# Sums of weight blocks in DRAM, requested at other places of a two-layer trunk kernel

## The chip, the cores and the metric

The kernel runs on one core of a Trainium2 chip. The metric is device time in microseconds of one execution. Three runs of the kernel before took 1001.95, 1002.94 and 1003.8 us (median 1002.94). A further execution was profiled: it took 1001.16 us, of which the trace covers a span of 999.4 us.

## The reference

Two layers, each a feed-forward block (FFN), a mixer and a second FFN, on 256 tokens of width 1024, all in float32:

```
def hybrid_layer(x, ...):
    x = x + 0.5 * swiglu(rms_norm(x, ffn1_norm), ffn1_w_gate_up, ffn1_w_down)
    z = rms_norm(x, mix_norm) @ w_in              # u, q, k, v, gates
    y_pool = multiscale_pool(u, pool_w, pool_scale)
    y_attn = moba_attention(rope(rms_norm(q)), rope(rms_norm(k)), v)
    gates = sigmoid(gl + b_gate)
    x = x + (gates[0] * (y_pool @ w_branch_pool) + gates[1] * (y_attn @ w_branch_attn)) @ w_out
    x = x + 0.5 * swiglu(rms_norm(x, ffn2_norm), ffn2_w_gate_up, ffn2_w_down)
    return x
```

An FFN's gate and up matrix is 1024 x 5632, its down matrix 2816 x 1024.

## The kernel before

**Weights.** They lie in DRAM as units of 1 MB, each used once. `fetch` (L134) loads the next unit of a fixed plan into one of four `raw` buffers with a DMA from SP's queue (L143, or L193 in `sum_form`). ScalarE (ACT) then rounds it to `hi` (L209, L198), and VectorE (DVE) makes the rest `lo` (L210, L199), in two halves each, since TensorE (PE) multiplies float32 as split float32r parts. There are three sets of hi and lo buffers. A load is thus issued when an earlier unit is split, and a split when PE has done with a still earlier one: PE, ACT, DVE and SP's queue form a ring some seven units deep.

**Stages.** In order of time, by the profile: FFN 1 of layer 0 (base 0, "the first stage") with 22 up units to about 129 us and 11 down units to 184; the mixer of layer 0 (`mix`: q, k and v units, the pooling input u in `project_u`, eight gate units, four branch units, four output units) to about 336; FFN 2 of layer 0 (base FU) to 509; FFN 1 of layer 1 (base LU) to 678; the mixer of layer 1 to 830; FFN 2 of layer 1 (base LU + FU) to the end.

**Seven products for eight.** The three FFNs after the first compute some of their up units by a scheme with seven products in place of eight, on groups A, B and C of units (`FEED`; FU and LU + FU have A and C in the order TWO, LU has A, B and C in the order THREE). Its forms "7", "6", "5" and "4" are sums of quarters of weight units. The names 1, 2 and 3 are plain quarters. PE's products with forms write tiles `b`; ordinary units write `ps`.

**The sums.** Each of the four forms of a group is made in DRAM by two DMAs from GpSimd's queue (POOL, L183), "steps" below: a copy of 1 MB into a DRAM tile `f` (from the weights `w`, or from another form: `f<-f`), then a second DMA that adds 1 MB onto it (`accum_op`). Form 6 starts from 7, and 4 from 6, so some steps wait until earlier ones have landed. Seven groups make 56 steps, of which 14 are `f<-f`. `far_sums` puts them into the list `steps_left`, the first eight steps of a group being interleaved with the last three (`rest`) of the group before, across the borders of the stages too. `go_on` (L175) takes the next step and issues it; it makes the DMA wait for the last entry of `marks`, the DVE instruction that ended the unit of work just before. So where `go_on` is called sets when a step may start, and POOL, which issues in order, may be held further by the landing of an earlier step. When the list is empty, `go_on` does nothing.

**Places before.** Seven calls among the up units of the first stage (after units 8, 10, ..., 20), five among the down units (`far_at`: units 1, 3, 5, 7, 9), and in the mixer one after q, two after the rotary steps of q and k, eleven at the gates (two after gates 0, 1 and 2, one after each other), two at branch units and four at output units: 20 in a mixer, 32 before FFN 2 of layer 0. That FFN has 4 + 5, the next 2 + 5, and the last 8 fall into the mixer of layer 1.

**Pooling on POOL.** `pool_sums` runs on POOL between the steps (L857 to L862); its result is first read by DVE in `pool_diff` (L868) after gate 3.

Of the kernel before, what the change touches and what calls it, by code (L numbers as in the profile page):

```python
# [44 lines left out]
FU = NF + NF // 2 + 24  # L45
LU = FU + NF + NF // 2
# [14 lines left out]
def groups_of(base):  # L61
    return "AC" if FEED[base] is TWO else "ABC"
# [12 lines left out]
C_G1, C_GM, C_G2, C_BG, C_PS, NG = 0, 8, 16, 24, 40, 44  # L75
# [3 lines left out]
def trunk_kernel(ctx: ExitStack, tc: tile.TileContext, x_in, w_in, pw_in, qkn_in, rope_in, mask_in, band_in, out):  # L79
    nc = tc.nc  # L80
# [31 lines left out]
    def banks(pool, name):  # L112

        return pool.tile([P, 2, 2, S], F32, name=name, tag="mm" if pool is pmm else "at2")
# [13 lines left out]
    def unit():  # L128

        if not ahead:  # L130
            fetch()
        return ahead.pop(0)
# [17 lines left out]
    far, steps_left = {}, []  # L150

    def quadrant(base, g, q):

        n, kh = base + GROUPS[g] + (0 if q[1] == "1" else 2), int(q[0]) - 1
        return w_in[n:n + 2, :, kh * HALF:(kh + 1) * HALF].rearrange("u p c -> p u c")

    def two_rows(z):
        return z.rearrange("p (i c) -> p i c", i=2)

    def far_sums():  # L160

        rest = []
        for base in STAGES:
            for g in groups_of(base):
                one, two = ({z[0]: (base, g, z[0], z[i], kw) for z in SUMS}
                            for i, kw in ((1, {}), (2, {"accum_op": OP.add})))
                for z in one["7"], one["5"], two["7"]:
                    steps_left.append(z)
                    steps_left.extend(rest[:1])
                    rest = rest[1:]  # L170
                steps_left.extend((two["5"], one["6"]))
                rest = [two["6"], one["4"], two["4"]]
        steps_left.extend(rest)

    def go_on():  # L175

        if not steps_left:
            return
        base, g, f, src, kw = steps_left.pop(0)
        if not kw:  # L180
            far[f, g, base] = far_pool.tile([P, 2 * HALF], F32, name="f" + f, tag=f"{base}{g}{f}")
        src = two_rows(far[src, g, base]) if len(src) == 1 else quadrant(base, g, src)
        z = nc.gpsimd.dma_start(two_rows(far[f, g, base]), src, **kw)  # L183
        tc.add_manual_dep(z.ins, marks[-1].ins.name, mybir.DependencyInfo(
            mybir.DependencyClass.Sync, mybir.DependencyReason.DATA), reason="behind")
# [60 lines left out]
    def pair(w, t, other=None, at=0):  # L246

        ps = banks(pmm, "ps")
        columns(w, ps, range(at))
        if other:  # L250
            other()
        columns(w, ps, range(at, NK))
        drain(t, ps)
# [8 lines left out]
    def behind(z, other):  # L262

        tc.add_manual_dep(z.ins, other.ins.name, mybir.DependencyInfo(
            mybir.DependencyClass.NoSync, mybir.DependencyReason.DATA), reason="behind")
# [22 lines left out]
    x = gx[:, L * NG:L * NG + NK * S].rearrange("p (k s) -> p k s", s=S)  # L288
# [18 lines left out]
    for t in range(PAD - 1):  # L307
        g = min(g for g, w in enumerate(WINDOWS) if t < w - 1)
# [7 lines left out]
    def split_x(f, l, col):  # L316

        g = gain[:, l, col + f:col + f + 1]
        act(hx[:, f, 0, :], x[:, f, :], AF.Copy, scale=g)
        stt(hx[:, f, 1, :], x[:, f, :], g, hx[:, f, 0, :].bitcast(F32), op0=OP.mult, op1=OP.subtract)  # L320

    def square_x(f):

        if f == 0:
            act(acc, x[:, f, :], AF.Square)
        else:
            sq = small.tile([P, S], F32, name="sq", tag="sq", bufs=2)
            act(sq, x[:, f, :], AF.Square)
            tt(acc, acc, sq, op=OP.add)

    def prep(f, l, col):
        split_x(f, l, col)
        square_x(f)
# [83 lines left out]
    def bc2(a):  # L417
        return a.unsqueeze(1).to_broadcast([P, 2, a.shape[-1]])

    def ffn(after, n0=0, end=False, col=None, base=0, far_at=(), steps_at=()):  # L420
# [19 lines left out]
        def wide(n):  # L440
            m = n // 2
            if m not in abs_:
                k = len(abs_)
                if n0 and 3 <= k < 7:
                    if not more:
                        z = acts.tile([P, NK * GW + 4 * SHIFT], F32, name="ab", tag="gates")
                        more.extend(z[:, i * 4 * S:(i + 1) * 4 * S].rearrange("p (b a s) -> p b a s", b=2, s=S) for i in range(4))
                    abs_[m] = more.pop(0)
                else:
                    abs_[m] = wide_tile(k if k < 3 or not n0 else k - 4)  # L450
            return abs_[m][:, n % 2]
# [25 lines left out]
        if n0:  # L477
# [6 lines left out]
            for i in range(n0 + 1, NF + 1):  # L484
                if i < NF:
                    pair(unit(), wide(i))
                    fetch()
                    if i >= 8 and i % 2 == 0:
                        go_on()
                if i == NF or i % 3 != 1:  # L490
                    for n in range(done, NF if i == NF else min(done + 2, i - 1), 2):
                        scaled = post(n)
                        done = n + 2
                        if i == n0 + 1:
                            behind(scaled, drained[-1])
# [206 lines left out]
    def normed(pt, rt, name):  # L702
        z = acts.tile([P, 2, GW], F32, name=name, **({"tag": "v"} if name == "v" else {"tag": "tok", "bufs": 2}))
        for t in range(2):
            act(z[:, t, :], pt[:, t], AF.Copy, scale=rt[:, t:t + 1])
        return z
# [87 lines left out]
    def mix(l, after):  # L794
# [5 lines left out]
        pt = tokens()  # L800
        r = spread(*z)
        k = normed(pt, rt, "k")
        spare = acts.tile([P, 8 * GW], F32, name="spare", tag="ga")
        yk, pk = ([z[:, i] for i in range(4)] for z in (
            acts.tile([P, 4, 2, S], F32R, name=n, tag=t) for n, t in (("yk", "gc"), ("pk", "gd"))))
# [23 lines left out]
        def project_u():  # L829
            us = [unit() for _ in range(2)]  # L830
            for g in range(0, NW, 2):
                ps = banks(pmm, "ps")
                for k in range(NK):
                    for j in range(2):
                        chain(ps[:, j], *us[k // 4], k % 4 * 4 + g + j, hk[k], k == 0, k == NK - 1)
                z = uT[:, g:g + 2, PAD:]
                drain(z, ps)
                tt(z, z, bc2(r), op=OP.mult)

        pool = [gates[6 + g // 2][:, g % 2, :] for g in range(NW)]  # L840
        W = PAD + S
# [57 lines left out]
        rest = slice(3 * P, 4 * P)  # L899
# [45 lines left out]
        for h in range(NH):  # L945
            gate(h, *((lambda: score_two(h // 2), NK // 2) if h % 4 == 0 else ()))
            if h == 4:
                for p, y in enumerate(ys):
                    heads_end(p, y)
                known = soften_two()  # L950
            elif h < 2:
                soften(h)
            elif h % 4 == 2:
                turn_two(h // 4 * 2, (0, 1) if h > 4 else ())
            elif h == 3:
                pool_diff()
            open_gate(h)
            for _ in range(2 if h < 3 else 1):
                go_on()

        def branch(f, j, k0=0, k1=4):
# [40 lines left out]
        for f in range(4, NK):  # L1002
            if f % 2 == 0:
                ws.append(unit())
                go_on()
            for j in range(2):
                branch(f, j)
            if f == 5:
                fetch()
            mixed(f)  # L1010
        ws, sums = [], []

        def project(f, k0=0, k1=NK):
            if f % 2 == k0 == 0:
                ws.append(unit())
                go_on()
            if k0 == 0:
                sums.append(quarter("ps"))
            ps = sums[f][:, 0]
            chain3(ps, *ws[f // 2], f % 2 * 8 + k0, mk[k0:k1], k0 == 0, k1 == NK)  # L1020
            if k1 == NK:
                marks.append(tt(x[:, f, :], ps, x[:, f, :], op=OP.add))
                after(f)
# [4 lines left out]
    w3 = [buffers() for _ in range(3)]  # L1028
# [20 lines left out]
    for l in range(L):  # L1049
        l_of[0] = l  # L1050
        if l == 0:
            far_sums()
        ffn(lambda f: prep(f, l, C_GM), len(w3) if l == 0 else 0, col=C_G1, base=l * LU, far_at=(1, 3, 5, 7, 9), steps_at=(2,))
        if l == 0:
            for d, z in ((rope, rope_in), (mask, mask_in), (qkn, qkn_in)):
                nc.sync.dma_start(d, z)
        mix(l, lambda f: prep(f, l, C_G2))
        if l + 1 < L:
            ffn(lambda f: prep(f, l + 1, C_G1), col=C_G2, base=FU, far_at=(1, 3, 5, 7, 9), steps_at=(3, 6, 10, 16))
        else:  # L1060
            ffn(lambda f: nc.sync.dma_start(out[:, f, :], x[:, f, :]), end=True, col=C_G2, base=LU + FU)


# [88 lines left out]
```

## Time and profile before

| | us |
|---|---|
| runs: lowest, median, highest | 1001.95, 1002.94, 1003.8 |
| profiled execution, its span | 1001.16, 999.4 |
| PE busy | 990.3 |
| PE weight loads busy | 898.5 |
| DVE busy | 805.5 |
| ACT busy | 654.9 |
| POOL busy | 62.7 |

PE is TensorE's matmuls and PEld its weight loads, which run beside them. A row of a wait view names the engine and the tile it was about to write, then what ended the idle time, the total in us, the count, and the longest. In a row of the timeline stand the start, the length, the engine, line, operation, tiles and count, and in brackets how long the engine had been idle and what ended it. A window row has the busy time of each engine with its count of instructions, TensorE's granted clock, the share of time that the 16 DMA engines were busy, and GB/s.

### The profile page before, as it was taken

The numbers are of one execution on the slowest core, as the hardware profiler recorded it, in microseconds if no ns is written. First come the engines' busy times: TensorE is split into PE (matmuls) and PEld (weight loads), VectorE is DVE, ScalarE is ACT, GpSimd is POOL, SyncE is SP. The second block draws the span as 40 slices with busy tenths as digits, with TensorE's granted clock in tenths as the row PEclk, the third lists the DMA queues.
The fourth block names the chain that finished last, engine by engine and source line by source line (L and its number), as shares of the span: only waits on it lengthen the run. The fifth ranks groups of instructions, "written<-read, shape, count | busy, mean of one in ns | idle before, by whom it ended". The sixth has DMA issues, their size and how long they took to land.

```text
span 999.4 us, 16133 instructions
## 1 busy us (share of the span) xinstructions
PE 990.3 (99%) x6304; PEld 898.5 (90%) x6304; DVE 805.5 (81%) x1141; ACT 654.9 (66%) x981; POOL 62.7 (6%) x103
## 2 busy tenths in 40 slices
PE   9999999999999989999999999999999999999998
PEld 8988999998899978889898889988988998888898
DVE  6987767698788689887689998876988788988862
ACT  7856555567666587775568877555677568776641
POOL 0000001003101000000000000000130000000000
PEclk9999999999999999999999999999999999999999
DMA  8879899958999989898969989887878665787740
GB/s 295 315 269 274 312 317 266 318 194 252 281 345 313 341 311 318 330 323 331 306 216 297 340 293 324 323 288 247 229 250 296 192 213 211 255 285 260 252 148 22
DMA packets 47756, 273.65 MB, mean 274 GB/s; under 512 B 4576, under 2 KB 5856, under 8 KB 24928
## 3 DMA queue, kind: packets, MB, share of 16 engines
q1 hardware_dynamic: 35808, 213.90, 58.2%
q0 software_dynamic: 11872, 58.72, 23.9%
q8 instruction: 49, 0.80, 0.3%
q14 instruction: 27, 0.22, 0.1%
HBM read 271.56 MB, written 59.77 MB: 332 GB/s over the span
## 4 chain that ended last, share of the span: by engine, by line
PE 94%; DMA 2%; DVE 2%; ACT 1%; issue 0%; SPq 0%; ACTq 0%
PE ps L110 66%; PE b L110 13%; PE pt L110 7%; PE two L110 4%; DMA raw<-w 2%; PE pe L110 1%; PE sc L110 1%; DVE lo L210 1%; PE pt L780 1%; PE y L110 1%; PE b L588 0%; PE tp L736 0%; ACT pre L529 0%; PE pt L588 0%; ACT hi L209 0%
## 5 line engine op out<-in xcount | busy, mean ns | idle before, releaser
L210 DVE TENSOR_TENSOR lo<-raw,hi 128x1024 fp32r<-128x1024 f32 (+2 forms) x311 | 368.4, 1197 | 109.0 <-ACT hi L209 106.7
L209 ACT ACTIVATE hi<-raw 128x1024 fp32r<-128x1024 f32 (+2 forms) x311 | 318.4, 1033 | 202.7 <-PE ps L110 114.7
L110 PE MATMUL ps<-hx,hi 128*128 128x512 f32 x1248 | 423.4, 385 | 2.1 <-DVE ab L259 1.5
L110 PE MATMUL ps<-hx,lo 128*128 128x256 f32 x1248 | 341.8, 274 | 0.0
L110 PEld LDWEIGHTS ps<-hx,hi 128*128 128x128 f32 x1248 | 235.0, 188 | 44.8 <-DVE ab L259 1.8
L110 PEld LDWEIGHTS ps<-hx,lo 128*128 128x128 f32 x1248 | 235.3, 189 | 0.2 <-DVE lo L210 0.2
L199 DVE TENSOR_TENSOR lo<-raw,hi 128x1024 fp32r<-128x1024 f32 x98 | 118.5, 1221 | 26.0 <-ACT hi L198 25.7
L198 ACT ACTIVATE hi<-raw 128x1024 fp32r<-128x1024 f32 x98 | 102.9, 1055 | 49.8 <-PE ps L110 19.3
L110 PE MATMUL ps<-ga,hi 128*128 128x512 f32 (+1 forms) x264 | 87.8, 378 | 0.0
L110 PE MATMUL b<-hi,sf 128*128 128x512 f32 x224 | 76.6, 383 | 0.0
L110 PE MATMUL ps<-ga,lo 128*128 128x256 f32 x256 | 70.0, 273 | 0.0
L183 POOL DMA_DIRECT2D f<-w x42 | 39.3, 981 | 482.8 <-DVE ab L259 219.7
L110 PE MATMUL ps<-gb,hi 128*128 128x512 f32 (+1 forms) x198 | 65.4, 376 | 0.0
L110 PE MATMUL pt<-hi,hx 128*128 128x512 f32 x192 | 64.9, 384 | 0.0
L110 PE MATMUL b<-lo,sf 128*128 128x256 f32 x224 | 61.5, 275 | 2.5 <-DVE lo L199 2.5
L110 PEld LDWEIGHTS ps<-ga,hi 128*128 128x128 f32 x264 | 49.0, 188 | 8.2
L110 PE MATMUL pt<-lo,hx 128*128 128x256 f32 x192 | 52.5, 274 | 0.0
L110 PE MATMUL ps<-gb,lo 128*128 128x256 f32 x192 | 52.4, 273 | 0.0
L110 PE MATMUL b<-hi,hx 128*128 128x512 f32 x168 | 51.8, 388 | 0.0
L110 PEld LDWEIGHTS b<-hi,sf 128*128 128x128 f32 x224 | 42.0, 188 | 7.4
L110 PEld LDWEIGHTS ps<-ga,lo 128*128 128x128 f32 x256 | 48.1, 188 | 0.0
L110 PEld LDWEIGHTS b<-lo,sf 128*128 128x128 f32 x224 | 42.0, 188 | 2.8 <-DVE lo L199 2.8
(214 smaller groups left out, 1577.0 us busy)
## 6 DMA issues: line engine op xcount, KB each, us to landing
raw<-w SPq DMA_DIRECT2D x169, 1024.0 KB, 7.1
f<-w POOLq DMA_DIRECT2D x42, 1024.0 KB, 12.9
raw<-f SPq DMA_DIRECT2D x28, 1024.0 KB, 6.7
raw<-w SPq DMA_DIRECT2D x16, 256.0 KB, 5.4
out_dram<-gx SPq DMA_DIRECT2D x8, 128.0 KB, 1.9
gx<-x SPq DMA_DIRECT2D x3, 256.0 KB, 5.8
qk<-pw SPq DMA_DIRECT2D x2, 256.0 KB, 3.8
gx<-x SPq DMA_DIRECT2D x1, 300.0 KB, 2.9
```

The source lines that it names most:

```text
L110: return keep(nc.tensor.matmul(*args, **kw))
L183: z = nc.gpsimd.dma_start(two_rows(far[f, g, base]), src, **kw)
L198: act(hv, a, AF.Copy)
L199: tt(lv, a, hv.bitcast(F32), op=OP.subtract)
L209: act(hi, w, AF.Copy)
L210: return tt(lo, w, hi.bitcast(F32), op=OP.subtract)
L780: keep(nc.tensor.transpose(pt[:, h, o * P:(o + 1) * P], pr[:, h, c * P:(c + 1) * P], ident))
```

## The change

The list of steps has the same 56 entries, with `rest` now emptied at the end of each stage instead of being carried into the next. The steps of FFN 2 of layer 0 are thus numbers 1 to 16, those of FFN 1 of layer 1 are 17 to 40, and those of FFN 2 of layer 1 are 41 to 56.

```
-        rest = []
         for base in STAGES:
+            rest = []
...
-        steps_left.extend(rest)
+            steps_left.extend(rest)
...
-                    if i >= 8 and i % 2 == 0:
+                    if i in (7,9,11,13,15,17,19,21):
                         go_on()
...
         k = normed(pt, rt, "k")
+        go_on()
...
                 tt(z, z, bc2(r), op=OP.mult)
+                if g in (0,2):
+                    go_on()
...
             open_gate(h)
-            for _ in range(2 if h < 3 else 1):
+            if h in (0,2,3,4,5,7):
                 go_on()
...
             if f % 2 == 0:
                 ws.append(unit())
-                go_on()
+                if f in (4,):
+                    go_on()
...
             if f % 2 == k0 == 0:
                 ws.append(unit())
-                go_on()
+                if f in (0,4):
+                    go_on()
...
-        ffn(..., far_at=(1, 3, 5, 7, 9), steps_at=(2,))
+        ffn(..., far_at=(1,3,5,7,9) if l else (0,2,4,6,8,10), steps_at=(2,))
```

The last FFN gets `steps_at=()`; its list is empty by then either way. The calls become 8 + 6 in the first stage (7 + 5 before) and 15 in a mixer (20 before): 3 until the rotary step of q, 1 after that of k, 2 in `project_u`, 6 at gates, 1 at a branch unit, 2 at output units. Before FFN 2 of layer 0 there are 29 calls (32 before), and by the mixer of layer 1 there are 45 (48 before), so 11 steps fall into that mixer (8 before).

The rows of PE, DVE, ACT and SP's queue are the same in both, but for line numbers, and numbers in names. POOL's rows differ at these places. First, POOL in the mixer of layer 0, around the start of `pool_sums`; a row `DMA f<-w` is a step (the number tells the DRAM tile). Before:

```order
L183 DMA f_1450<-w 256x1x1024
L183 DMA f_1344<-w 256x1x1024
L183 DMA f_1957<-f_1147 16x16384
L183 DMA f_2092<-w 256x1x1024
L183 DMA f_1957<-w 256x1x1024
L858 TENSOR_TENSOR gates<-uT 128x256
L857 TENSOR_TENSOR spare<-uT 128x3x271
L857 TENSOR_TENSOR spare<-spare 128x2x269
```

The last three of these steps are the ones after q's work, after q's rotary step and after k's. In the changed kernel, the same place:

```order
L183 DMA f_1960<-f_1698 16x16384
L183 DMA f_1960<-w 256x1x1024
L183 DMA f_2096<-w 256x1x1024
L183 DMA f_2215<-w 256x1x1024
L183 DMA f_2096<-w 256x1x1024
L861 TENSOR_TENSOR gates<-uT 128x256
L183 DMA f_2215<-w 256x1x1024
L860 TENSOR_TENSOR spare<-uT 128x3x271
L860 TENSOR_TENSOR spare<-spare 128x2x269
```

All six DMA rows now lie between the first stage's end and `pool_sums`; the sixth stands between the first and the second instruction of `pool_sums` and adds onto `f_2215`, which the row four above it copies.

Second, POOL from the end of `pool_sums` in layer 0's mixer, through the gates, branches and outputs. Before, the first 12 of the 17 steps up to FFN 2:

```order
L862 TENSOR_TENSOR spare<-spare,uT 128x64
L183 DMA f_2418<-w 256x1x1024
L183 DMA f_2420<-f_1957 16x16384
L183 DMA f_2092<-w 256x1x1024
L183 DMA f_2420<-w 256x1x1024
L183 DMA f_2418<-w 256x1x1024
L183 DMA f_2551<-f_2092 16x16384
L183 DMA f_2606<-w 256x1x1024
L183 DMA f_2551<-w 256x1x1024
L183 DMA f_2759<-w 256x1x1024
L183 DMA f_2833<-f_2551 16x16384
L183 DMA f_2606<-w 256x1x1024
```

In the changed kernel, all nine up to FFN 2, and the first of that FFN:

```order
L865 TENSOR_TENSOR spare<-spare,uT 128x64
L183 DMA f_2425<-f_2096 16x16384
L183 DMA f_2553<-w 256x1x1024
L183 DMA f_2425<-w 256x1x1024
L183 DMA f_2711<-w 256x1x1024
L183 DMA f_2761<-f_2425 16x16384
L183 DMA f_2553<-w 256x1x1024
L183 DMA f_2761<-w 256x1x1024
L183 DMA f_2711<-w 256x1x1024
L183 DMA f_3335<-f_2553 16x16384
L183 DMA f_3780<-w 256x1x1024
```

Seventeen steps between `pool_sums` and FFN 2 have become nine.

More of the change, by code (lines that the diff above doesn't have):

```diff
@@ L1052, in trunk_kernel @@
             far_sums()
-        ffn(lambda f: prep(f, l, C_GM), len(w3) if l == 0 else 0, col=C_G1, base=l * LU, far_at=(1, 3, 5, 7, 9), steps_at=(2,))
+        ffn(lambda f: prep(f, l, C_GM), len(w3) if l == 0 else 0, col=C_G1, base=l * LU,
+            far_at=(1,3,5,7,9) if l else (0,2,4,6,8,10), steps_at=(2,))
         if l == 0:
@@ L1058, in trunk_kernel @@
         if l + 1 < L:
-            ffn(lambda f: prep(f, l + 1, C_G1), col=C_G2, base=FU, far_at=(1, 3, 5, 7, 9), steps_at=(3, 6, 10, 16))
+            ffn(lambda f: prep(f, l + 1, C_G1), col=C_G2, base=FU, far_at=(1,3,5,7,9), steps_at=(3,6,10,16))
         else:
-            ffn(lambda f: nc.sync.dma_start(out[:, f, :], x[:, f, :]), end=True, col=C_G2, base=LU + FU)
+            ffn(lambda f: nc.sync.dma_start(out[:, f, :], x[:, f, :]), end=True, col=C_G2, base=LU + FU, steps_at=())
 def _feat(a):
```

## The prediction, made before the changed kernel ran

> **What bounds the kernel now.** I read the page's busy times first, then who waited for whom on TensorE, the chain of waits around the longest wait, and the windows, each stage of layer 0 beside the same stage of layer 1.
>
> ```profile
> PE 990.3 (99%) x6304; PEld 898.5 (90%) x6304; DVE 805.5 (81%) x1141; ACT 654.9 (66%) x981; POOL 62.7 (6%) x103
> DMA  8879899958999989898969989887878665787740
> ```
>
> PE is busy 990.3 of 999.4 us, and the change leaves PE's instructions as they are. So it can take away only PE's 9.1 us of idle time, and it can add waits without such a limit. The second row says that the DMA engines are nearly full for long stretches, while the last quarter has room.
>
> The weight loads' wait view tells where the idle time is. I use PEld rather than PE, since the ends of matmuls are modelled.
>
> ```profile
> PEld b L110 <- DVE lo L199: 2.8, 1, 2.8
> PEld ps L110 <- DVE ab L259: 1.8, 1, 1.8
> PEld busy L110 <- DVE eps L298: 1.1, 1, 1.1
> PEld ps L110 <- ACT hi L209: 0.9, 1, 0.9
> ```
>
> The last two belong to the start, before the first weights are there, and stay. The other two, 2.8 + 1.8 = 4.6 us, are the whole prize. The chain of waits (start, length, what) shows where they lie and what stands ahead of them.
>
> ```profile
> 320.70 1.14 DVE lo L210
> 321.89 19.11 DMA raw<-w
> 341.05 0.32 issue
> 341.37 1.06 ACT hi L198
> ...
> 365.16 1.15 DVE lo L199
> 366.35 1.40 PE b L110 x7
> ```
>
> PE waits at 366 in the first product of a form in FFN 2 of layer 0. Ahead of it ACT and DVE work without a break from 341 on, and that work began late because a load of 1 MB took 19.11 us. The windows tell whether this is a property of the stage. The first two rows are the output units of layer 0's mixer and the FFN after them up to its last transposed tile; the other two are the same work in layer 1.
>
> ```profile
> 305.70:335.70 30.00, 30.00 (x242) 29.19 (x241) 23.76 (x42) 18.56 (x31) 3.33 (x4) 1.00 1.04 311
> 335.70:454.60 118.90, 114.88 (x689) 102.65 (x689) 100.86 (x125) 85.97 (x117) 5.92 (x7) 1.00 0.94 322
> 799.80:829.80 30.00, 30.00 (x243) 29.19 (x242) 23.77 (x42) 18.67 (x31) 0.00 (x0) 1.00 0.63 211
> 829.80:944.10 114.30, 114.30 (x690) 102.61 (x689) 105.24 (x125) 86.87 (x117) 0.00 (x0) 1.00 0.72 253
> ```
>
> The same PE work takes 118.9 us in layer 0 and 114.3 in layer 1: again 4.6 us. The clock is 1.00 in all four. What differs is the DMA share, 1.04 against 0.63 in the 30 us ahead of the FFN, and POOL's steps (last engine column), which layer 1 has not. Loads there, from the DMA view of two windows, 285 to 345 and 799 to 839 us (count, size, median us from issue to landing):
>
> ```profile
> raw<-w SPq DMA_DIRECT2D x9, 1024.0 KB, 14.9
> f<-w POOLq DMA_DIRECT2D x8, 1024.0 KB, 19.4
> raw<-w SPq DMA_DIRECT2D x7, 1024.0 KB, 5.2
> ```
>
> A load that takes 5.2 us without steps takes 14.9 beside them (first and last row). **So the steps' backlog makes PE wait.** Its making is in POOL's timeline:
>
> ```profile
> 128.68 0.67 POOL L183 DMA_DIRECT2D f<-w  x1 [4.11 <-DVE ab L259]
> 188.00 0.52 POOL L183 DMA_DIRECT2D f<-f  x1 [14.97 <-DVE gx L676]
> 222.44 1.05 POOL L183 DMA_DIRECT2D f<-w  x1 [11.67 <-DVE k L730]
> 252.10 2.10 POOL L183 DMA_DIRECT2D f<-w  x2 [5.39 <-DMA f<-f]
> 309.45 2.11 POOL L183 DMA_DIRECT2D f<-w  x2 [8.18 <-DVE th L970]
> 319.24 0.52 POOL L183 DMA_DIRECT2D f<-f  x1 [7.68 <-DMA f<-w]
> 338.44 1.76 POOL L183 DMA_DIRECT2D f<-w  x2 [17.96 <-DMA f<-f]
> 364.85 0.50 POOL L183 DMA_DIRECT2D f<-f  x1 [24.66 <-DVE ab L259]
> ```
>
> At the gates eleven steps are asked for in some 45 us. From 252 on a step goes out only when an earlier one has landed (`<-DMA f<-w`), and the steps of the branch and output units queue behind them until 338, inside the FFN.
>
> **The change, part by part.** One step's price comes from the page:
>
> ```profile
> q1 hardware_dynamic: 35808, 213.90, 58.2%
> q0 software_dynamic: 11872, 58.72, 23.9%
> ```
>
> q0 carries the 56 steps: 0.239 x 999.4 / 56 = 4.3 us of all 16 engines for one. q1 carries 204 MB-loads (213.90 / 1.0486): 0.582 x 999.4 / 204 = 2.85 us for one. These are shares under contention, so what follows from them is an estimate. The windows of the places that gain steps are (the third is the gates of layer 1):
>
> ```profile
> 118.00:184.00 66.00, 66.00 (x399) 59.41 (x398) 47.91 (x67) 36.28 (x52) 5.52 (x7) 1.00 0.94 290
> 184.00:241.00 57.00, 57.00 (x356) 51.15 (x355) 46.63 (x80) 34.14 (x52) 9.55 (x13) 1.00 0.74 247
> 736.00:790.00 54.00, 54.00 (x407) 49.81 (x407) 43.97 (x73) 40.22 (x80) 3.98 (x5) 1.00 0.81 254
> ```
>
> *Gates, branches, outputs (what is removed).* From 285 to 345 ten steps went out (the eight of the middle row above and two `f<-f`); four of the new fifteen fall there (gate 7, branch unit 4, outputs 0 and 4). The DMA share falls from the 1.04 quoted by 6 x 4.3 / 60 = 0.43 to 0.61, near layer 1's 0.63. No step is then in flight from about 330 until the FFN's first own step, so the FFN's first loads land in about 5 us in place of 19, and ACT and DVE begin at 327 or so what they began at 341. Both waits go: **-4.6 us**. What is late next is nothing that layer 1's twin stage shows: it has the same ACT and DVE work and no wait. At the FFN's end the step count is 38 in place of 41, and the three go to the mixer of layer 1.
>
> *First stage (added).* Eight steps go out from 118 to 184 in place of six: 0.94 + 2 x 4.3 / 66 = 1.07, full. Three of them come at once: the calls after up unit 21 and at down units 0 and 2 all wait for the same drain of unit 21, near 128.7. What hides this is the ring's depth:
>
> ```profile
> 127.81 0.33 SPq L143 DMA_DIRECT2D raw<-w  x1
> 144.12 1.06 ACT L209 ACTIVATE hi<-raw 128x1024 fp32r<-128x1024 f32 x1 [0.17 <-ACT sq L328]
> ```
>
> By counting loads, the one issued at 127.81 is split from 144.12 on: 16.3 us, and none of ACT's waits from 118 to 184 is for a DMA. Its unit is the 7th of the down units, which PE begins 6 x 5.34 us after 128.7, at 160.7, some 11 us after the split's end near 149. A load would thus have to take over 27 us. The longest load of the trace's crowded stretch took about 19. Cost 0; bounds 0 and, if a 19 us load there cost PE as much as the one in the chain, 4.6. I take 0, since the nearest rows are those of this place.
>
> *Mixer of layer 0 to 241 us (added).* Six steps in place of three: 0.74 + 3 x 4.3 / 57 = 0.97. By the same count the loads there have 7 to 15 us between landing and split. One step is put ahead of most of `pool_sums` on POOL and waits until the step of 222.44 has landed; behind it stand `pool_sums` and the steps of the gates, and for `pool_sums` DVE waits at L868:
>
> ```profile
> 238.89 0.32 POOL L862 TENSOR_TENSOR spare<-spare,uT 128x64 f32<-128x64 f32 x1
> 256.80 1.43 DVE L868 SCALAR_TENSOR_TENSOR uT<-gates,uT 128x256 f32<-128x256 f32 x4
> ```
>
> There are 256.80 - 239.2 = 17.6 us between them. `pool_sums` begins at 232.3 after uT is complete; a copy issued at 222.44 that takes the 13.1 us of the trace's step at that place lands at 235.5 and delays it by some 4 us. Cost 0; it would begin to cost from a landing after 249. Bounds 0 and about 2 us (a step of 28.8 us, the longest).
>
> *Mixer of layer 1.* Eleven steps in place of eight, at places 494 us later: 0.81 + 3 x 4.3 / 54 = 1.05 at most, but behind it lies a stretch at 0.63 that has no step at all. Layer 0 had eleven at the gates alone and PE did not wait there. Cost 0, bounds 0 and 2.
>
> *Readiness of the sums.* FFN 2 of layer 0 has its 16 steps out soon after 188 (numbers 15 and 16 are the calls after q and after k), some 140 us before its first form. The last two of FFN 1 in layer 1 go out at about 521 and 529, and its last form is loaded near 600. Cost 0.
>
> **Sum.** 1001.16 - 4.6 = 996.5 us for a profiled execution. Runs without the profile have a median 1.8 us above it, so on their scale 1002.94 - 4.6 = **998.3 us**.
>
> **Rivals.**
>
> *The wait moves along.* All 56 steps remain. The Trainium skill, "DMA: Bandwidth & Descriptors", section "Issuing engines are not separate DMA queues", says that DMAs of every queue end up on the same 16 engines and interleave. By that alone nothing is saved. The trace bears it out: the loads slow from 5.2 to 14.9 us when steps run. But it has places with a share of 0.74, 0.63 and 0.72. If the wait comes again elsewhere, the time is 1002.9; if one of the two waits stays, because ACT and DVE, both busy from 341 to 366, need more than the earlier start gives, it is 1001.1 or 1000.1.
>
> *The form "5" in FFN 2 of layer 0 arrives late (slower).* Layer 1 shows its margin: the load's issue, its split on ACT, and PE's product:
>
> ```profile
> 854.37 0.33 SPq L193 DMA_DIRECT2D raw<-f  x1
> 860.68 1.06 ACT L198 ACTIVATE hi<-raw 128x1024 fp32r<-128x1024 f32 x1 [2.37 <-DVE ab L468]
> 870.71 2.68 PE b L110 x16
> ```
>
> The split is done 5.1 us after it begins, so a load of over 870.71 - 5.1 - 854.37 = 11.2 us makes PE wait. In layer 0 the FFN's first step (after up unit 3, at 364.85 before, 4.6 us earlier in the change) goes out just then. A load of 14.9 us costs 3.7 and leaves a gain of 0.9; at 15.8 the gain is gone; at 19.1 it costs 7.9, 3.3 more than is won: 1006.2 us. Against it: this is a single step, and the next is called only after up unit 6. The Trainium skill, same page, section "Queues, rings and completion order", says that a DMA engine goes round its queues packet by packet. By that rule a load beside any number of steps takes at most about twice its 5.2 us, 10.4 (an estimate), and this rival would cost nothing; the 14.9 us row differs from it.
>
> *The runs gain more than the profile shows.* Timed runs lie 1.8 us above the profiled one. If that is more of the same wait, it goes too: 1001.16 - 4.6 = 996.5.
>
> **Chances.** Both waits gone, as summed: 0.56. More gained: 0.12, 996.5. One of the two stays: 0.10, half of it on either side of the bound. The wait stays or moves: 0.12, 1002.9. Slower by the form's load: 0.10. A measurement of this kernel can tell about 0.2%, 2.0 us. So faster 0.56 + 0.12 + 0.05 = 0.73, same 0.17, slower 0.10. The range reaches from 996.0 to 1001.5, from the larger gain to the case in which only the smaller wait goes; about 0.2 lies outside.
>
> **What would show it.** Right: no PEld wait of over 1 us after the start; loads of about 5 us from 310 to 360; a DMA share near 0.6 from 285 to 345; the FFN's window at 114.3. Wrong: a wait of `b` or `ps` near 376 for a load of form 5, an ACT wait for DMA between 128 and 184 that passes on to PE, DVE idle at L868 for POOL, or the two waits as before with loads of 5 us, which would make ACT and DVE the cause.

## The result, and the profile after

| | runs, median (lowest to highest, count) | profiled execution | its span |
|---|---|---|---|
| before | 1002.61 us (1001.95 to 1003.80, 4) | 1001.16 us | 999.4 us |
| after | 995.66 us (994.96 to 997.37, 4) | 995.92 us | 994.2 us |

The ratio is 0.9932, with a 95% interval of 0.9915 to 0.9949. The forecast was 998.3 us, from 996.0 to 1001.5. The sign and the place were as foretold; the time lies 0.3 us below the range. A second comparison, told below, measured 995.38 against 1000.94 us: a ratio of 0.9940 [0.9926, 0.9954], or 5.6 us.

First, the page's busy times and its DMA row in 40 slices, of the kernel after.

```profile
PE 988.2 (99%) x6304; PEld 896.9 (90%) x6304; DVE 807.3 (81%) x1141; ACT 655.5 (66%) x981; POOL 64.4 (6%) x103
DMA  8889899989979769899979889898799565787740
```

The thirteenth to the fifteenth digit (298 to 373 us), which were 9, 9, 8, are 9, 7, 6. PE has the same 6304 products; its busy time is 2.1 us less, 1.4 of them in the start. PEld's waits after:

```profile
PEld ps L110 <- ACT hi L209: 1.7, 1, 1.7
PEld sc L110 <- issue: 1.3, 6, 0.2
PEld busy L110 <- DVE eps L298: 1.1, 1, 1.1
PEld ps L110 <- DVE gates L259: 0.4, 2, 0.2
```

The waits of 2.8 and 1.8 us are gone. The rest are the waits of 1.7 and 1.1 us in the start, which the change doesn't touch, and waits of at most 0.3 us. The windows (bounds, then busy time of PE, PEld, DVE, ACT and POOL, granted clock, DMA share, GB/s) of the places the prediction spoke of:

```profile
118.00:184.00 66.00, 66.00 (x397) 59.39 (x397) 47.42 (x66) 36.11 (x53) 6.61 (x9) 1.00 0.98 308
184.00:241.00 57.00, 57.00 (x355) 51.17 (x355) 47.39 (x79) 33.54 (x50) 13.47 (x16) 1.00 0.94 291
285.00:345.00 60.00, 60.00 (x477) 58.18 (x476) 50.13 (x88) 38.16 (x59) 2.59 (x3) 1.00 0.85 259
334.80:449.11 114.31, 114.31 (x690) 102.64 (x689) 101.61 (x126) 86.26 (x117) 3.98 (x5) 1.00 0.85 288
736.00:790.00 54.00, 54.00 (x422) 50.34 (x421) 45.58 (x73) 38.20 (x73) 3.13 (x4) 1.00 0.84 266
```

PE is busy in all of each window, the FFN of layer 0 up to its last transposed tile among them (fourth row). PE's `ss` tiles mark the ends of the stages. First the kernel after (rows of the chain of waits: start, length), then the kernel before (rows of PE's timeline):

```profile
334.80 0.23 PE ss L110 x2
...
508.78 0.23 PE ss L110 x2
```

```profile
335.53 0.39 PE L110 MATMUL ss<-ar,one_r 128*128 128x256 f32 x2
...
514.08 0.39 PE L110 MATMUL ss<-ar,one_r 128*128 128x256 f32 x2
```

From one to the other, FFN 2 of layer 0 with the start of the next FFN, are 173.98 us. The kernel before took 178.55, so the difference is 4.57 us of the 5.2 us of the two spans. Of the other 0.6, the start and the stages ahead gave 0.9, and the two stages of layer 1 behind it took 0.2 back (315.81 us against 315.59). I use this stage, "FFN 2's stage", as the measure in the experiments. In every kernel whose PE doesn't wait there it is 173.98 us to the hundredth.

The loads from 285 to 345 us and the steps issued then, in the DMA view (count, size, median us to landing):

```profile
raw<-w SPq DMA_DIRECT2D x9, 1024.0 KB, 8.6
f<-w POOLq DMA_DIRECT2D x2, 1024.0 KB, 13.1
```

The loads fell from 14.9 to 8.6 us, not to 5. The load that took 19.11 us in the chain before, issued at 321.89, takes 7.61 here, issued at 321.01. ACT's split of it, at 341.37 before, begins at 334.83, so 5.7 us earlier counted from `ss`. POOL's timeline (start, length, and in brackets its idle time before and what ended that):

```profile
128.18 0.68 POOL L183 DMA_DIRECT2D f<-w  x1 [4.82 <-DVE ab L259]
128.80 0.57 POOL L183 DMA_DIRECT2D f<-f  x1
129.28 1.17 POOL L183 DMA_DIRECT2D f<-w  x1
...
239.13 0.32 POOL L865 TENSOR_TENSOR spare<-spare,uT 128x64 f32<-128x64 f32 x1
...
283.43 1.06 POOL L183 DMA_DIRECT2D f<-w  x1 [11.14 <-DVE gates L259]
...
317.91 0.53 POOL L183 DMA_DIRECT2D f<-f  x1 [10.74 <-DVE gx L1027]
...
357.55 0.68 POOL L183 DMA_DIRECT2D f<-w  x1 [39.11 <-DVE ab L259]
```

From 283 on each step goes out when DVE asks for it, no longer when an earlier step has landed. None goes out between 318 and 357. `pool_sums` ends at 239.45, as before (239.21), so the step put ahead of it held it up by 0.2 us, with 17.6 us to spare.

### The profile page after: what moved, and what is told of

Read it like the earlier page. It is cut to its first block, busy times and chain, and to the rows that moved or that the text cites. A ratio compares the mean times of both kernels' runs of the same rounds, so it can differ in the third digit from the quotient of the medians.

```text
span 994.2 us, 16135 instructions
## 1 busy us (share of the span) xinstructions
PE 988.2 (99%) x6304; PEld 896.9 (90%) x6304; DVE 807.3 (81%) x1141; ACT 655.5 (66%) x981; POOL 64.4 (6%) x103
## 4 chain that ended last, share of the span: by engine, by line
PE 99%; DMA 0%; ACT 0%; DVE 0%; SPq 0%; issue 0%
PE ps L110 70%; PE b L110 13%; PE pt L110 7%; PE two L110 4%; PE pe L110 1%; PE sc L110 1%; PE pt L780 1%; PE y L110 1%; DMA raw<-w 0%; PE b L588 0%; PE tp L736 0%; PE pt L588 0%; PE st L110 0%; PE ss L110 0%; ACT hi L209 0%; DVE gx L684 0%
## 5 line engine op out<-in xcount | busy, mean ns | idle before, releaser
L110 PE MATMUL ps<-gc,hi 128*128 128x512 f32 (+1 forms) x132 | 44.2, 376 | 0.0
```

The lines of the kernel that those rows point to most:

```text
L110: return keep(nc.tensor.matmul(*args, **kw))
```

## The experiments

Each kernel was timed beside the kernel before on the same chip, in three groups; the kernel before had medians of 1001.40 (32 runs), 1000.94 (21) and 1000.82 us (16) in them.

**The kernel before, once more.** Nothing was edited. It asks where the 1.8 us between its first profile and its runs came from.

> The kernel before, unchanged, to see how large its wait is in another execution. Theory (the timed runs of the kernel before carry more of the same wait than its profiled run): the new profile shows PEld waits in FFN 2 of layer 0 whose sum W varies, and span minus W is again about 994.8 us (999.4 - 4.6); in a run of 1002.6 us W is about 6. Rival (what the timed runs have more lies at the start or around the span): W is 4.6 again within 0.5 us and span minus W moves with the run.

Measured: 1001.42 us (12 runs), ratio 1.0001 [0.9990, 1.0013]. The profiled execution took 1002.69 us, and its mean granted clock was 0.998, where before's first profile has 1.000. PEld's waits:

```profile
PEld b L110 <- DVE lo L199: 3.3, 1, 3.3
PEld ps L110 <- DVE ab L259: 0.4, 1, 0.4
```

Windows around the longer one, with the clock after the brackets of POOL:

```profile
361.90:365.30 3.40, 0.39 (x4) 0.09 (x2) 3.40 (x7) 3.40 (x5) 0.50 (x1) 0.94 1.08 389
365.30:368.30 3.00, 3.00 (x10) 2.62 (x11) 3.00 (x3) 3.00 (x5) 0.00 (x0) 0.50 0.21 63
368.30:372.00 3.70, 3.70 (x24) 3.32 (x24) 3.70 (x6) 1.19 (x2) 0.00 (x0) 1.00 0.84 312
```

And two of PE's rows from its timeline:

```profile
365.63 0.63 PE L110 MATMUL b<-hi,sf 128*128 128x512 f32 x1
...
368.57 0.39 PE L110 MATMUL ps<-hx,hi 128*128 128x512 f32 x1
```

My expectation was that the runs simply wait longer. This one doesn't: the waits sum to 3.7 us, less than the 4.6 of the first profile, while the span without them is 997.2 us where I expected 994.8. One part of these 2.4 us is that the granted clock falls to 0.50 when PE has stood idle, and for 3.0 us after the idle stretch a matmul of the same shape takes 0.63 us in place of 0.39. That costs half of the 3.0 us. FFN 2's stage took 179.03 us, 5.05 more than 173.98: 3.7 of waiting and 1.4 of low clock. Another part has nothing to do with a wait. In FFN 1 of layer 1 the same 310 products of the down units took 1.5 us longer than in the first profile (first row here, second row there), at a granted clock of 1.00 and with PE busy throughout; why stays open.

```profile
627.09 53.15 PE ps L110 x310
```

```profile
626.77 51.67 PE ps L110 x310
```

Of the kernel before's 69 runs in the three groups, 48 show a mean clock of 0.998 or less, as this one does; the first profile was one of the minority. (A mean of 0.999 also occurs in the kernel after, so I don't count it as a fall.) **So what a wait costs PE here is often more than the wait.**

**The late places as before.** The changed kernel with the calls at gates, branches and outputs of the kernel before (17 in place of 9), so that one part is undone.

```diff
-            if h in (0,2,3,4,5,7):
+            for _ in range(2 if h < 3 else 1):
                 go_on()
...
-                if f in (4,):
-                    go_on()
+                go_on()
...
-                if f in (0,4):
-                    go_on()
+                go_on()
```

> The changed kernel with its early calls, but the calls at gates, branch units and output units as before (17 in place of 9). Theory (the backlog made at the gates and after makes PE wait): the DMA share from 285 to 345 us is 1.0 again, loads there take 13 to 19 us, PE waits 4 to 8 us in FFN 2 of layer 0, time 1000 to 1003 us. Rival (the earlier start and the new order of the steps bring the gain): no such wait, 995 to 997 us.

Measured: 998.97 us (10 runs), ratio 0.9973 [0.9962, 0.9985]. DMA view from 285 to 345, and the waits:

```profile
raw<-w SPq DMA_DIRECT2D x9, 1024.0 KB, 13.5
```

```profile
PEld b L110 <- ACT tk L611: 2.2, 1, 2.2
PEld b L110 <- DVE lo L199: 1.8, 1, 1.8
```

The crowding is back, and with it 4.0 us of waiting in FFN 2 (stage 177.88 us). Of the two waits only that for `lo` is one of the kernel before; that for `tk` is new, and the experiment with three steps explains it. The time is above that of the kernel after, but 2.4 us below before's and below the 1000 us that I expected at least. The waits come as two gaps of some 2 us; only 1 of 10 runs has a mean clock of 0.998, and the stage had no fall in the profile.

**The gates alone, and the branches and outputs alone, as before.** Two kernels, each with a part of the edit above.

> The changed kernel with only the gate calls as before (11 in place of 6), branch and output units as changed (3). Theory A (the calls at branch and output units matter, being next to the FFN): the backlog is gone by about 310 us, no wait of PE, 995 to 997 us. Theory B (the gates make the backlog and it lasts): loads of over 12 us up to 340, PE waits 2 to 5 us, 998 to 1001 us.

> The changed kernel with the calls at branch and output units as before (6 in place of 3), gates as changed. The gate calls alone cost a wait of 1.1 us. Theory A (a step right ahead of the FFN costs more than one at the gates): waits of 1.5 us or more, 997 to 999 us. Theory B (only the sum of both makes a backlog; three more steps alone fit): no wait, within 1 us of the changed kernel.

Eleven gate calls: 997.00 us (7 runs), 0.9954 [0.9937, 0.9971], a wait of 1.1 us in FFN 2, stage 175.21. Six branch and output calls: 995.90 us (4 runs), 0.9950 [0.9935, 0.9964], no wait, stage 173.98. So with the new early places the six calls of the tail cost nothing that is measured (theory B of the second kernel), the gates' five extra ones about 1.2 us in the profile (a wait, but less than theory B of the first had), and both together 3.9: the surplus must add up before PE feels it. The loads from 285 to 345 us in the kernel with six tail calls, and its window there, show how much PE bears:

```profile
raw<-w SPq DMA_DIRECT2D x9, 1024.0 KB, 13.2
```

```profile
285.00:345.00 60.00, 60.00 (x477) 58.18 (x476) 47.75 (x84) 36.95 (x58) 5.07 (x6) 1.00 0.95 295
```

These loads are about as slow as the 13.5 us of the kernel with both edits, and ACT waits up to 2.8 us for one (up to 5.5 in the kernel before), yet PE never waits. Slow loads in that stretch are thus not enough by themselves.

**The new order of the steps alone.** The kernel before, with only the reordered list.

```diff
-        rest = []
         for base in STAGES:
+            rest = []
...
-        steps_left.extend(rest)
+            steps_left.extend(rest)
```

> The kernel before with only the list's new order (rest emptied at each stage's end), all calls where they were. Theory: as before, PE waits 4 to 8 us in FFN 2 of layer 0, 1001 to 1004 us. Rival (the order brings the gain, since POOL is held less by steps that must land first): 995 to 998 us.

Measured: 1000.13 us (10 runs), ratio 0.9986 [0.9972, 1.0000]. Both waits are there (2.8 and 1.9 us), with a fall of the clock, and the stage took 180.16 us. The order isn't where the gain comes from: the median lies 0.9 us below the 1001 us that I expected at least, and whether the order gives even that is not shown, as the interval reaches 1.0000. Five runs with a mean clock of 0.998 have a median of 1001.21, the five with 1.000 have 999.42 us.

**The late cut alone.** The kernel after with the early calls of the kernel before; the five steps left over are called after down units of FFN 2 in layer 0.

```diff
-                    if i in (7,9,11,13,15,17,19,21):
+                    if i >= 8 and i % 2 == 0:
...
-        go_on()
...
-                if g in (0,2):
-                    go_on()
...
-            far_at=(1,3,5,7,9) if l else (0,2,4,6,8,10), steps_at=(2,))
+            far_at=(1,3,5,7,9), steps_at=(2,))
...
-            ffn(lambda f: prep(f, l + 1, C_G1), col=C_G2, base=FU, far_at=(1,3,5,7,9), steps_at=(3,6,10,16))
+            ffn(lambda f: prep(f, l + 1, C_G1), col=C_G2, base=FU, far_at=(1,2,3,4,5,6,7,8,9,10), steps_at=(3,6,10,16))
```

> The changed kernel's order and its calls at gates, branch and output units, but the first stage and the start of the mixer as before (12 + 3 calls in place of 14 + 6); the five calls that are then missing go to the down units of FFN 2 of layer 0 (all of 1 to 10). Theory (taking steps away from the gates and after is all that counts; the earlier places only find room for them): no wait, stage 174.0 us, 995 to 996.5 us. Rival (the early places are needed): waits in FFN 2 of layer 0 or in FFN 1 of layer 1, 997 us or more.

Measured: 999.41 us (7 runs), ratio 0.9979 [0.9965, 0.9993]. FFN 2's stage is 173.98, without a wait. My theory had no wait at all and 996.5 us at most; the rival, that the early places are needed, came out. FFN 1 and the mixer of layer 1 took 319.14 us together in place of 315.81. The wait there, and the steps ahead of it on POOL:

```profile
PEld b L110 <- ACT tk L611: 3.6, 1, 3.6
```

```profile
510.45 1.02 POOL L183 DMA_DIRECT2D f<-w  x1 [18.55 <-DMA f<-f]
525.73 0.53 POOL L183 DMA_DIRECT2D f<-f  x1 [14.25 <-DMA f<-w]
533.48 1.02 POOL L183 DMA_DIRECT2D f<-w  x1 [7.22 <-DVE sf L538]
```

`<-DMA f<-f` is the sign of a backlog, as at 252 us in the kernel before. PE's idle 3.3 us from 507 to 560 (first row; the second is the kernel after) lie in the next FFN, so the crowd has moved there:

```profile
507.00:560.00 53.00, 49.71 (x298) 44.35 (x297) 45.17 (x60) 41.52 (x60) 2.57 (x3) 1.00 0.97 330
```

```profile
507.00:560.00 53.00, 53.00 (x320) 47.46 (x319) 49.08 (x65) 45.91 (x63) 1.55 (x2) 1.00 0.85 289
```

The late cut frees FFN 2 by itself. But the steps must go out somewhere: at FFN 2's down units five of them cost 3.3 us in the next FFN, while in the first stage and the mixer's beginning they cost nothing.

**Three steps beside the load of form 5.** The kernel after, with three calls in place of one after up unit 3 of FFN 2 in layer 0; it tests the slower rival.

```diff
-                    go_on()
+                    for _ in range(3 if base == FU and n == 3 else 1):
+                        go_on()
```

> The changed kernel with three calls after up unit 3 of FFN 2 of layer 0 in place of one, when the load of form 5 is in flight. Theory (my margin: a load of form 5 of over 11.2 us makes PE wait, and steps in a row make it that long): that load takes 11 to 15 us, PE waits 0.5 to 4 us at the b product after the fifth up unit, 996.5 to 1000 us. Rival (the queues share by turns, so three steps slow one load no more than one does): load under 11 us, no wait there.

Measured: 1001.10 us (10 runs), ratio 0.9998 [0.9989, 1.0007]; the whole gain is lost. The timeline of POOL, ACT and PE:

```profile
356.97 2.47 POOL L183 DMA_DIRECT2D f<-w  x3 [39.11 <-DVE ab L259]
```

```profile
371.32 1.06 ACT L198 ACTIVATE hi<-raw 128x1024 fp32r<-128x1024 f32 x1 [6.51 <-DMA raw<-f]
...
376.50 2.00 ACT L209 ACTIVATE hi<-raw 128x1024 fp32r<-128x1024 f32 x2 [2.17 <-DMA raw<-w]
```

```profile
379.04 0.79 PE L110 MATMUL b<-hi,sf 128*128 128x512 f32 x1 [3.94 <-ACT tk L611]
```

The load of form 5 took 12.7 us, that of the next unit 15.7; in the kernel after they took 8.7 and 8.9. PE waits for neither by name. It waits for ACT's copy of the product `tk` out of its bank, and ACT stands before that copy at the split of the *next* unit's load (second row), which landed late. The wait is 4.2 us, the stage 179.65: 4.2 and another 1.4 of low clock. All ten runs show a low mean clock (0.996 to 0.998). The load of form 5 was as expected (11 to 15 us); the wait and the time are a little more than expected (at most 4 us and 1000 us).

**A gap by itself.** Three kernels put one gap into the last FFN of the kernel after, where the rest has slack: PE's next matmul after up unit 6 waits for ACT's copy (e8), or for POOL's memset and one (e6) or six adds (e7) of a small tile that nothing reads.

```diff
+                if base == LU + FU and n == 6:
+                    w = small.tile([P, S], F32, name="hold", tag="hold", bufs=1)
+                    z = nc.gpsimd.memset(w, 0.0)
...
+                    for _ in range(1):
+                        z = nc.gpsimd.tensor_tensor(w, w, w, op=OP.add)
+                    held.append(z)
```

> The changed kernel with one idle time of TensorE put in by hand: in FFN 2 of layer 1 the first product after up unit 6 also waits for a short chain on GpSimd that starts when unit 6 is drained (a memset and one addition). Nothing of the result changes. Idle time about 2 to 2.8 us. Theory (the clock falls only after an idle time near 3 us or more): the clock stays at 1.00, the stage grows by the idle time alone. Rival (any such idle time costs more than itself): the clock falls to 0.5 for some us after it.

> As the short one, with six additions: idle time about 5 to 6 us. Theory: the clock falls to 0.5 for about 3.4 us, and the stage grows by the idle time plus 1.2 to 1.7 us. Rival (the fall seen in the kernel before has another cause, such as the state of the chip): the clock stays at 1.00 and the stage grows by the idle time alone.

> The changed kernel, with the first product after up unit 6 of FFN 2 of layer 1 waiting for ACT's copy of unit 6 out of PSUM, which needs no GpSimd: an idle time of about 2.1 us at the place where 4.56 us made the clock fall. Theory (an idle time of some 2 us leaves the clock alone, as 1.1, 1.8 and 2.2 us did in the runs so far): clock 1.00 to the end, the stage 166.37 + 2.1 us, 997 to 998 us. Rival (it falls at this place whatever the length): clock 0.5 for 3.4 us or more, 999 us or more.

| | gap, us | low clock, us | last stage: first `ss` to the end of PE's last product (166.37 without a gap) | beyond the gap | median us, ratio |
|---|---|---|---|---|---|
| e8 | 2.11 | none | 168.63 | 0.15 | 999.07, 0.9981 [0.9970, 0.9992] |
| e6 | 4.56 | 6.83 | 173.87 | 2.94 | 1002.38, 1.0009 [1.0000, 1.0018] |
| e7 | 8.01 | 10.24 | 177.43 | 3.05 | 1005.52, 1.0040 [1.0027, 1.0054] |

The gap meant to be short came out at 4.56 us, so e8 was made for the short case; and in e7 the low clock lasted three times the 3.4 us that I expected. The windows of e6, and the last row of e7:

```profile
864.30:868.90 4.60, 0.34 (x3) 0.05 (x1) 4.03 (x5) 2.57 (x4) 0.92 (x2) 0.89 0.80 253
868.90:874.70 5.80, 5.80 (x18) 4.92 (x19) 1.23 (x1) 1.26 (x2) 0.00 (x0) 0.50 0.38 158
874.70:880.00 5.30, 5.30 (x33) 4.70 (x32) 3.45 (x4) 2.80 (x4) 0.00 (x0) 1.00 0.42 100
```

```profile
872.10:878.20 6.10, 6.10 (x19) 5.23 (x20) 1.23 (x1) 1.53 (x2) 0.00 (x0) 0.50 0.00 0
```

A gap after which the clock falls costs its own length and half of the low-clock time in which PE works: 5.8 / 2 = 2.9 and 6.1 / 2 = 3.05 us, as measured. In e8's profile the clock stayed, and the gap cost its length. Even so the median is 1.1 us above the expected 998, 3 of its 10 runs show a mean clock of 0.998, and their median is 1000.07 against 998.08 of the other seven. These three runs have no trace, so that their clock fell after the gap of 2.1 us is likely, not shown.

**The kernel after, once more.** Nothing was edited.

> The changed kernel, unchanged. Theory (besides 4.6 us of waits, the kernel before loses about 1.4 us in most executions because TensorE's granted clock falls to 0.5 for 3.41 us after the idle time; with no wait there is no fall): no PEld wait over 1 us after the start, no fall of the clock inside the span, FFN 2 of layer 0 (first ss to next ss) 174.0 us again, nearly all runs at clock 1.000, and 5 to 6.5 us less than the kernel before. Rival (the runs of the first comparison were lucky): waits or falls of the clock in this profile, or less than 4.6 us gained.

Measured: 995.38 us (5 runs), ratio 0.9940 [0.9926, 0.9954], no wait in FFN 2, stage 173.98, no fall ahead of the end of PE's work. This is the better measure of the change, since the kernel before has 21 runs beside it.

## Why the prediction was right in its mechanism and off in its size

**The cause: right.** It said that the steps' backlog at the gates slows the loads, and that this makes PE wait in FFN 2. Undoing the late cut brought back 13.5 us loads and 4.0 us of waiting; making it alone took the wait of that stage away. Two readings went too far. Not every step from 252 on waited for a landing: of POOL's seven idle times there up to 339, four end with a landing and three with DVE. And slow loads don't decide it alone, since with 13.2 us loads and six tail calls PE didn't wait.

**Both waits go, -4.6 us: right.** FFN 2's stage lost 4.57 us from the first profile to that of after, and from its `ss` to its last transposed tile it is the foretold 114.3 us with PE busy throughout. The way there was not quite the foretold one. The load landed at 328.6 us, near the foretold 327, but ACT began its split only at 334.83, as the splits ahead of it now wait for PE to free buffers. So ACT began 5.7 us earlier and not 14, and that was enough.

**The added steps cost nothing: right.** The three from 128.2 us on slowed the next four loads, of 4.9 to 7.9 us before, to 10.0 to 12.0; ACT has no wait for a DMA from 118 to 184 us, as the ring's depth promised. `pool_sums` was foretold some 4 us late and was 0.2 late: the step it would have waited for had landed by 229.7. DVE never waited at the pooling sums, and layer 1's mixer has no new wait.

**"Runs without the profile have a median 1.8 us above it, so on their scale 1002.94 - 4.6": this is the step that failed.** It carried the 1.8 us over as a constant that the change leaves alone. The kernel after has no such excess: the median of its runs lies 0.3 us below its profiled execution (995.66 against 995.92). On the profile's own scale the sum, 996.5 us, was near. In place of the constant the runs showed two things, and a rest stays open.

- *The three runs shown lay high.* Their median was 1002.94 us, while the 69 later runs of the same kernel have 1001.11, from 998.92 to 1004.91. Only 19 of the 69 reach the lowest of the three, 1001.95. This 1.8 us is most of the miss of 2.7, and the later runs don't have it. Those three runs have no trace, so where their time lay stays open. The profiled executions show parts that vary whatever the change: the time until the first `ss`, from 29.7 to 32.1 us, and the 1.5 us of slower products in FFN 1 of layer 1.
- *The price of a wait was mis-sized.* I priced each wait at its length, as the first profile showed it. In most executions the clock also falls after it: the stage then lost 3.7 + 1.4 = 5.05 us in the profile taken again, against 4.57 in the first. The 48 runs with a mean clock of 0.998 or less have a median of 1001.40 us, the 21 others 1000.73, so a low clock goes with 0.7 us more, or 0.5 us on average over all runs (an estimate). It goes when the wait goes: all nine runs of the kernel after have a mean clock of 0.999 or 1.000.

The second comparison's gain is 5.6 us, from 4.6 to 7.4 by its interval. The waits' 4.6 and the 0.5 make 5.1; whether the remaining 0.5 is longer waits in untraced runs or chance is not shown. The rival "the runs gain more than the profile shows", with 996.5 us and a chance of 0.12, came nearest. Its reason, more of the same waiting, is not borne out by the execution profiled again, which waited 3.7 us.

The Trainium skill has the rule in "TensorE: Matmul & The Clock Gate", section "Part 1: The HAM clock gate (the "warmup" mystery)": the clock halves after an idle window of about 3.4 us, and the windows run freely. The traces agree in the lengths (3.41, 6.83 and 10.24 us are one, two and three windows), in the half clock and in the free run, as the last section works out. They differ in that a window need not be idle throughout: PE was busy for 0.41 of one after which the clock fell.

**DMA shares: the size was wrong.** From 285 to 345 the share is 0.85, where the sum of step prices gave 0.61, and the loads took 8.6 us, not 5. The price of 4.3 us for one step is not what failed. The steps moved 9.16 MB in that stretch before and 4.19 after, so by bytes 4.7 steps of 1.05 MB went away and not six; what was left cost 5.0 us of all engines per step (33.7% of 60 us) where it had been 4.0, and the loads moved 0.84 MB more. The other three estimates, 1.07, 0.97 and 1.05 at most, came out at 0.98, 0.94 and 0.84. Of the four signs named for being right, the share near 0.6 thus didn't come, and loads of about 5 us from 310 to 360 only for forms (5.3; plain units took 7.0). None of it changed the time, since PE had more room than the sum assumed.

**The form-5 rival: real, but at another place.** I set its margin at a load of 11.2 us for form 5 itself. In the kernel with three steps that load took 12.7 us, and PE waited 4.2 us, where 12.7 - 11.2 = 1.5 was expected. The binding load is the next unit's, through ACT's order: split of the next load first, then the copy of `tk`. In three kernels PE's product starts 2.6 us after that load has landed: at 375.59 after 372.94 with eleven gate calls (1.1 us of wait), at 377.96 after 375.32 with the late places as before (2.2), at 379.04 after 376.40 with three steps (4.2). In the kernel after the load landed at 370.18, 5.3 us before the product at 375.51, and there is no wait. The changed kernel's margin at this place is thus 5.3 - 2.6 = 2.7 us.

The prediction weighed this rival against a rule of the Trainium skill, "DMA: Bandwidth & Descriptors", section "Queues, rings and completion order": queues take turns packet by packet. From it the prediction worked out that any number of steps slows a load to at most about twice its time alone. That bound, 10.4 us, doesn't hold here: with one step beside them these two loads took 8.7 and 8.9 us and with three 12.7 and 15.7, while their twins in layer 1, without steps, took 6.8 and 7.0. The second is thus slowed to more than twice its twin too.

## What to carry to other kernels

Read the granted clock around each wait of TensorE, and over several executions: here a low clock went with the waits in most executions (1.4 us on top of 3.7 in the one that was profiled), and one profile in which the clock happened to stay hid it. Don't add the distance between three runs and one profile to a forecast as a constant: here it was mostly the spread of the runs. Where background transfers can go out at many places, look whether a step waits for an earlier one to land, which is the sign of a backlog, and which load is in flight beside it: three steps that waited only for their caller lost the whole gain when they met the load of form 5. A cut at one end needed room at another. When an in-order engine splits loads and also empties PSUM, a late load can show up as TensorE waiting for that engine's copy of something else, so follow the engine's order back to the load before setting a margin.

## What the runs showed of the chip that I had not expected

- The granted clock fell to 0.50 in steps of 3.41 us after idle time of PE: for 3.41 us after gaps of 3.3 and 4.2 us, 6.83 after 4.56, 10.24 after 8.01. The fall began inside the gap, so only 3.0, 5.8 and 6.1 us of PE's work ran slow. Gaps of 1.8 and 2.8 us close together ended without a fall in one profile of the kernel before, and gaps of 1.9 and 2.8 with one in the kernel with the new order alone; a gap of 3.6 us in the kernel with the late cut alone had none.
- Where a gap lies in time decides what it costs, as far as these traces show. In their clock records the stretches at full clock are whole multiples of 3.413 us too (631.47 us, 185 of them, from the end of the low stretch to the next fall in the kernel before profiled again), so the clock goes by a fixed grid. Laid over PE's rows, the windows of this grid after which the clock fell had PE busy for 0.00, 0.00, 0.04, 0.23 and 0.41 of their length; every other window at full clock between the start and the end of PE's work had 0.46 or more. The gap of 3.6 us without a fall is cut in two by the grid, with 0.54 and 0.49 busy; the 2.8 us of the first profile lie in a window with 0.47. A gap of 2.1 us that falls into one window leaves it 0.38 busy (an estimate: 1.3 of 3.41 us), which would fit the three low runs of e8.
- A step of 1 MB on POOL's queue doesn't cost the loads beside it a fixed share: the median load took 5.2 us without steps, 8.6 with few of them, 14.9 in a backlog.
